# Two joining copies moved behind a weight's casts in ScalarE's queue

## The chip, the core and the metric

The kernel runs on one core of a Trainium2 chip. A core has five engines, each with its own queue of instructions that it takes in order: TensorE (PE; its weight loads are listed apart as PEld), VectorE (DVE), ScalarE (ACT), GpSimd (POOL) and SyncE (SP), which issues the DMA transfers here. Engines wait for one another by semaphores. The metric is the device time of one execution in microseconds (us); lower is better.

## The reference

Two layers of a decoder trunk for 512 tokens of width 1024, in fp32. Each layer has a feed-forward sub-layer, a mixing sub-layer (three kinds of attention, gated and merged) and a second feed-forward sub-layer, all with normalisation before and after:

```
def _swiglu(t, w_gate, w_up, w_down):
    return (jax.nn.silu(t @ w_gate) * (t @ w_up)) @ w_down

for l in range(DEPTH):
    f = _swiglu(_rmsnorm(h, ffn1_pre_g[l]), ffn1_w_gate[l], ffn1_w_up[l], ffn1_w_down[l])
    h = h + 0.5 * _rmsnorm(f, ffn1_post_g[l])
    ...   # mixing
    f = _swiglu(_rmsnorm(h, ffn2_pre_g[l]), ffn2_w_gate[l], ffn2_w_up[l], ffn2_w_down[l])
    h = h + 0.5 * _rmsnorm(f, ffn2_post_g[l])
```

The hidden width of the feed-forward sub-layers is 2816, 22 columns of 128. The change concerns these four feed-forward stages only. In the kernel their names carry `a` (the first of a layer) or `c` (the second).

## The kernel before

**Three matmuls for one.** Every fp32 operand is split into a high part (`wh_...`, `ah...`: rounded to fp32r) and a low part (`wl_...`, `al...`: the rest), and a product is three matmuls: high by high, low by high, high by low (`mm3`, lines 205 to 207). The high part is a cast on ScalarE and the low part a subtraction on VectorE that needs the cast (`split`, lines 182 and 183). The split of a weight tile of 128x1024 is thus a DMA into a raw tile (`raw_...`), a cast and a subtraction. High parts have a ring of four buffers and low parts another ring of four.

**Seven products for eight.** Sixteen of the 22 hidden columns are handled as two blocks (numbers 0 and 1) by a scheme with seven products of half size where eight would be needed. A gate job, an up job and a down job exist for each block and product. A down job (ci, n) is product n of block ci. It has two weight units (`wh_dc_1_1_0` and `wh_dc_1_1_2` are the units of job (1,1) in stage `c`: rows from 0 and from 2), each used by 12 matmuls, so a job is 24 matmuls. The down jobs run in the order

(0,0), (1,0), (0,1), (1,1), (0,2), (1,2), (0,3), (0,4), and so on,

which makes (0,1) the third and (1,1) the fourth. In between stand passes over the six remaining hidden columns, two columns to a weight, one column to a pass of 24 matmuls. Around the change the order on TensorE is: (1,0), gate pass of column 18, (0,1), (1,1), gate pass of column 19, (0,2), up pass of column 18, (1,2). The weights of the two gate passes are the same two units, which hold two of the four buffers until the second pass is over.

**Turning the hidden values.** The up products of a block give a hidden quarter with tokens and features the other way round from what the down jobs need. `turn` (line 796) turns it with the DMA engine, two bytes at a time: two copies on ScalarE part each word into halves (line 807, tiles `th...`), two transposing DMAs turn the halves (line 808, into `tr...`), and two *joining copies* on ScalarE put the words together again in the tile of hidden rows (line 811, into `hr...`). `turn` is called from each later product job. It parts the words in the first job after the quarter is done and joins them two or three jobs later. The last up product of block 1 (product 6) fills the second token half of `hr..._2`. Its joining copies are traced in job (1,1).

**Who needs the joined tile.** The left factor of a down job is a sum of hidden quarters on VectorE, then split (`first_factor`, lines 845 to 851). Line 845 for (1,2), `as..._1_2`, is the first reader of the joined half. The left factor is made one job ahead.

**What sets the order.** The code is traced in the order in which jobs are stepped through, with weights of up to four units loaded ahead of the running job. A scheduler then orders each engine's queue by data dependences and its own estimate of when each instruction is ready. `tc.keep_in_program_order` pins an instruction to the traced order, and `tc.issue_after(ins)` queues what is traced inside it behind `ins` on that engine; it adds an order, not a wait for `ins` to end.

## Time and profile before

| | us |
|---|---|
| median of 3 runs | 2356.36 |
| lowest, highest | 2354.06, 2357.69 |
| the profiled execution, its time | 2354.76 |
| its span on the core | 2353.0 |
| TensorE busy in the span | 2339.6 (99%) |
| VectorE busy | 1798.8 (76%) |
| ScalarE busy | 1505.3 (64%) |

The granted TensorE clock is 0.999 of full speed over the span. A row of a time line has the start in us from the span's start, the duration, the engine, the line, the operation, out<-in by tile names with the buffer numbers left out, the shape, and a count when neighbours of one kind are merged; a bracket gives the idle time of that engine just before, and what ended it. Matmuls overlap, so a duration of 0.39 does not mean that the next one starts 0.39 later: the starts tell the pace.

### The profile page before, as it was taken

How to read it: one execution, taken by the hardware profiler on the slowest of the kernel's cores; microseconds unless marked ns; L12 is line 12 of the kernel's file. 1: busy time of each engine (PE TensorE's matmuls, PEld its weight loads, DVE VectorE, ACT ScalarE, POOL GpSimd, SP SyncE). 2: the span in 40 equal slices, each digit the busy share in tenths (PEclk: the TensorE clock that was granted, in tenths of full speed). 3: DMA queues.
4: the chain of work that ended last, by engine and by line, in shares of the span. 5: the costliest groups of instructions: out<-in, count | busy, mean ns of one | idle time of the engine just before them, and what ended most of it. 6: DMA issues, size and time to landing. Idle time of an engine off the chain costs nothing.

```text
span 2353.0 us, 30931 instructions
## 1 busy us (share of the span) xinstructions
PE 2339.6 (99%) x11623; PEld 1977.7 (84%) x11623; DVE 1798.8 (76%) x2359; ACT 1505.3 (64%) x2302; POOL 75.5 (3%) x134
## 2 busy tenths in 40 slices
PE   9999999999999999999999999999999999999998
PEld 7888888888888888878898888888888888988887
DVE  8877876577777688878798788766677767888785
ACT  6677465576766556774656774655777665667744
POOL 0000000000111000000000000000001100000000
PEclk9999999999999999999999999999999999999999
DMA  6667454223323555674646655532323235566744
GB/s 206 192 178 220 143 197 129 78 83 88 91 72 108 188 188 159 199 188 153 225 145 182 202 176 178 189 108 72 100 72 99 73 124 190 170 189 181 207 145 146
DMA packets 297849, 354.96 MB, mean 151 GB/s; under 512 B 78282, under 2 KB 189154, under 8 KB 297700
## 3 DMA queue, kind: packets, MB, share of 16 engines
q1 hardware_dynamic: 297604, 352.97, 48.8%
q8 instruction: 91, 1.49, 0.3%
q14 instruction: 58, 0.48, 0.1%
q0 software_dynamic: 96, 0.03, 0.0%
HBM read 319.39 MB, written 16.78 MB: 143 GB/s over the span
## 4 chain that ended last, share of the span: by engine, by line
PE 90%; DMA 4%; DVE 2%; ACT 2%; issue 1%; SPq 0%; DVEq 0%; ACTq 0%
PE pg L206 4%; PE pg L205 4%; PE pg L207 4%; PE pda L206 3%; PE pdc L206 3%; PE pda L205 3%; PE pda L207 3%; PE pdc L207 3%; PE pdc L205 3%; PE pb L207 1%; PE pb L206 1%; PE pb L205 1%; PE pq L205 1%; PE pq L206 1%; PE pk L207 1%
## 5 line engine op out<-in xcount | busy, mean ns | idle before, releaser
L205 PE MATMUL pg<-us_a,wh_wg 128*128 128x512 f32 x384 | 151.1, 394 | 0.0
L206 PE MATMUL pg<-us_a,wh_wg 128*128 128x512 f32 x384 | 149.9, 390 | 0.0
L207 PE MATMUL pg<-us_a,wl_wg 128*128 128x512 f32 x384 | 149.9, 390 | 0.0
L183 DVE TENSOR_TENSOR wl_da<-raw_da,wh_da 128x1024 fp32r<-128x1024 f32 x50 | 61.0, 1224 | 46.3 <-ACT wh_da L182 46.1
L183 DVE TENSOR_TENSOR wl_dc<-raw_dc,wh_dc 128x1024 fp32r<-128x1024 f32 x50 | 61.0, 1223 | 44.5 <-ACT wh_dc L182 44.4
L206 PE MATMUL pdc<-wl_dc,ahc 128*128 128x512 f32 x224 | 88.0, 393 | 1.5 <-DVE wl_dc L183 1.5
L206 PE MATMUL pda<-wl_da,aha 128*128 128x512 f32 x224 | 88.0, 393 | 0.3 <-DVE wl_da L183 0.3
L207 PE MATMUL pdc<-wh_dc,alc 128*128 128x512 f32 x224 | 87.3, 390 | 0.0
L207 PE MATMUL pda<-wh_da,ala 128*128 128x512 f32 x224 | 87.3, 390 | 0.0
L205 PE MATMUL pdc<-wh_dc,ahc 128*128 128x512 f32 x224 | 86.7, 390 | 0.4 <-ACT wh_dc L182 0.4
L205 PE MATMUL pda<-wh_da,aha 128*128 128x512 f32 x224 | 86.6, 390 | 0.0
L207 PEld LDWEIGHTS pg<-us_a,wl_wg 128*128 128x128 f32 x384 | 72.1, 188 | 15.1
L205 PEld LDWEIGHTS pg<-us_a,wh_wg 128*128 128x128 f32 x384 | 72.2, 188 | 14.1
L206 PEld LDWEIGHTS pg<-us_a,wh_wg 128*128 128x128 f32 x384 | 72.2, 188 | 14.0
L182 ACT CAST wh_da<-raw_da 128x1024 fp32r<-128x1024 f32 x50 | 52.2, 1049 | 41.5 <-DMA raw_da<-in_ffn_w_down_dram 13.6
L182 ACT CAST wh_dc<-raw_dc 128x1024 fp32r<-128x1024 f32 x50 | 52.1, 1049 | 36.5 <-DMA raw_dc<-in_ffn_w_down_dram 12.2
L186 DVE SCALAR_TENSOR_TENSOR wl_wg<-raw_wg,wh_wg 128x1024 fp32r<-128x1024 f32 x48 | 58.5, 1222 | 21.9 <-ACT wh_wg L185 21.8
L200 DVE SCALAR_TENSOR_TENSOR ga<-pg,bgate,ga 128x512 f32<-128x512 f32 x48 | 35.9, 747 | 50.0 <-ACT ga L199 50.0
L182 ACT CAST wh_uc<-raw_uc 128x1024 fp32r<-128x1024 f32 x44 | 46.3, 1053 | 39.8 <-PE pwc0g L207 9.4
L183 DVE TENSOR_TENSOR wl_uc<-raw_uc,wh_uc 128x1024 fp32r<-128x1024 f32 x44 | 53.7, 1221 | 17.1 <-ACT wh_uc L182 16.9
L185 ACT ACTIVATE wh_wg<-raw_wg 128x1024 fp32r<-128x1024 f32 x48 | 50.5, 1056 | 25.1 <-PE pv L1113 11.7
L182 ACT CAST wh_ua<-raw_ua 128x1024 fp32r<-128x1024 f32 x44 | 46.2, 1052 | 31.1 <-PE pwa0g L207 8.1
(643 smaller groups left out, 8017.3 us busy)
## 6 DMA issues: line engine op xcount, KB each, us to landing
raw_da<-in_ffn_w_down_dram SPq DMA_DIRECT2D x66, 512.0 KB, 4.7
raw_dc<-in_ffn_w_down_dram SPq DMA_DIRECT2D x66, 512.0 KB, 4.3
raw_ga<-in_ffn_w_gate_dram SPq DMA_DIRECT2D x52, 512.0 KB, 4.5
raw_ua<-in_ffn_w_up_dram SPq DMA_DIRECT2D x52, 512.0 KB, 4.7
raw_gc<-in_ffn_w_gate_dram SPq DMA_DIRECT2D x52, 512.0 KB, 4.0
raw_uc<-in_ffn_w_up_dram SPq DMA_DIRECT2D x52, 512.0 KB, 4.0
raw_wg<-in_w_gate_dram SPq DMA_DIRECT2D x48, 512.0 KB, 3.6
raw_wo<-in_w_out_dram SPq DMA_DIRECT2D x24, 512.0 KB, 3.4
```

The source lines that it names most:

```text
L182: both = [nc.scalar.copy(h_ap, src)]
L183: make = lambda: nc.vector.tensor_tensor(l_ap, src, h_ap.bitcast(F32), ALU.subtract)
L185: both = [nc.scalar.activation(h_ap, src, AF.Copy, scale=scale)]
L186: make = lambda: nc.vector.scalar_tensor_tensor(l_ap, src, scale, h_ap.bitcast(F32), ALU.mult, ALU.subtract)
L200: nc.vector.scalar_tensor_tensor(t, z, minus, t, ALU.max, ALU.add)
L205: nc.tensor.matmul(pt, lh, rh, start=start, stop=False, skip_group_check=free)
L206: nc.tensor.matmul(pt, lh, rl, start=False, stop=False, skip_group_check=free)
L207: nc.tensor.matmul(pt, ll, rh, start=False, stop=stop, skip_group_check=free)
```

## The change

The joining copies of the last up product of block 1 (hidden rows 2, second token half) are traced inside `tc.issue_after` of the high part's cast of the last unit of down job (1,1). For this `split` returns its instructions, a unit keeps its cast in `self.cast`, and `products` keeps the last unit of (1,1) in `st["second"]`. All other joining copies stay as they were. Nothing is added to or taken from the program; the order changes in all four feed-forward stages in the same way.

```diff
@@ def split @@
         if Q.pinned:
             for ins in both:
                 tc.keep_in_program_order(ins)
+        return both
@@ class BlockUnit @@
-            self.heir, self.behind = None, False
+            self.heir, self.behind, self.cast = None, False, None
...
-            self.split_from(src)
+            self.cast = self.split_from(src)[0]
             self.loaded()
@@ def turn @@
                 if kk in (0, 1) and age == back:
                     r = hidden_rows(row)[:].bitcast(U16)
-                    nc.scalar.copy(r[:, :, i * S + kk:(i + 1) * S:2].rearrange("p f (e q) -> p e f q", e=2),
-                                   planes[kk].rearrange("p (e f q) -> p e f q", e=2, q=P))
+                    dst_ = r[:, :, i * S + kk:(i + 1) * S:2].rearrange("p f (e q) -> p e f q", e=2)
+                    src_ = planes[kk].rearrange("p (e f q) -> p e f q", e=2, q=P)
+                    last = (row, i) == (2, 1)
+                    with tc.issue_after(st["second"].cast.ins) if last else nullcontext():
+                        nc.scalar.copy(dst_, src_)
@@ def products @@
                 had[ci, n] = uns
+                if (ci, n) == (1, 1):
+                    st["second"] = uns[-1]
                 yield uns, (lambda at=at, uns=uns: product(at, uns))
```

ScalarE's queue in the second feed-forward stage of the first layer, before. `hrc_2` is the joined tile, `trc0u_6_*` the turned halves, `sc_18` the activated gate of column 18, `btc` a kept weight block.

```order
L182 CAST ahc_0_2_9438<-asc_0_2_9440 128x1024
L811 COPY hrc_2_9047<-trc0u_6_0_9316 128x2x4x128
L811 COPY hrc_2_9047<-trc0u_6_1_9317 128x2x4x128
L630 ACTIVATE sc_18_9575<-pgc_18_9350 128x512
L182 CAST wh_dc_1_1_0_9340<-raw_dc_1_1_0_9252 128x1024
L182 CAST wh_dc_1_1_2_9346<-raw_dc_1_1_2_9254 128x1024
L182 CAST wh_dc_0_2_0_9377<-btc_0_0_9286 128x1024
```

And after the change (lines have moved by up to six):

```order
L182 CAST ahc_0_2_9438<-asc_0_2_9440 128x1024
L631 ACTIVATE sc_18_9575<-pgc_18_9350 128x512
L182 CAST wh_dc_1_1_0_9340<-raw_dc_1_1_0_9252 128x1024
L182 CAST wh_dc_1_1_2_9346<-raw_dc_1_1_2_9254 128x1024
L816 COPY hrc_2_9047<-trc0u_6_0_9316 128x2x4x128
L816 COPY hrc_2_9047<-trc0u_6_1_9317 128x2x4x128
L182 CAST wh_dc_0_2_0_9377<-btc_0_0_9286 128x1024
```

The activation and the two casts of (1,1) went ahead of the two copies.

VectorE's queue at the same place, before. `asc_1_2` is the sum that reads the joined tile, `asc_0_2` the running sum of block 0, `alc` a low part of a left factor.

```order
L183 TENSOR_TENSOR wl_dc_1_1_0_9341<-raw_dc_1_1_0_9252,wh_dc_1_1_0_9340 128x1024
L183 TENSOR_TENSOR alc_0_2_9439<-asc_0_2_9440,ahc_0_2_9438 128x1024
L845 TENSOR_TENSOR asc_1_2_9510<-hrc_2_9047,hrc_3_9006 128x1024
L183 TENSOR_TENSOR wl_dc_1_1_2_9347<-raw_dc_1_1_2_9254,wh_dc_1_1_2_9346 128x1024
L327 TENSOR_TENSOR btc_0_0_9286<-btc_0_0_9286,raw_dc_0_2_0_9288 128x1024
L847 TENSOR_TENSOR asc_0_2_9440<-asc_0_2_9440,hrc_0_8445 128x1024
L183 TENSOR_TENSOR wl_dc_0_2_0_9378<-btc_0_0_9286,wh_dc_0_2_0_9377 128x1024
```

And after:

```order
L183 TENSOR_TENSOR wl_dc_1_1_0_9341<-raw_dc_1_1_0_9252,wh_dc_1_1_0_9340 128x1024
L183 TENSOR_TENSOR alc_0_2_9439<-asc_0_2_9440,ahc_0_2_9438 128x1024
L851 TENSOR_TENSOR asc_0_2_9440<-asc_0_2_9440,hrc_0_8445 128x1024
L183 TENSOR_TENSOR wl_dc_1_1_2_9347<-raw_dc_1_1_2_9254,wh_dc_1_1_2_9346 128x1024
L328 TENSOR_TENSOR btc_0_0_9286<-btc_0_0_9286,raw_dc_0_2_0_9288 128x1024
L849 TENSOR_TENSOR asc_1_2_9510<-hrc_2_9047,hrc_3_9006 128x1024
L183 TENSOR_TENSOR wl_dc_0_2_0_9378<-btc_0_0_9286,wh_dc_0_2_0_9377 128x1024
```

The sum that reads the joined tile and the subtraction of block 0's running sum have changed places. On TensorE one matmul of the following gate pass moves ahead of the first low-part matmul of the second unit of (1,1). Further on, ScalarE and VectorE each swap one split of an activation with one of a weight. The queues of SyncE and GpSimd are the same.

More of the change, by code (lines that the diff above doesn't have):

```diff
@@ L1 @@
 import itertools
-from contextlib import ExitStack, contextmanager
+from contextlib import nullcontext, ExitStack, contextmanager
 import concourse.bass as bass
```

## The prediction

> **What bounds the kernel now.** I read the page's busy times first, then TensorE's waits, then time lines of ScalarE, VectorE and TensorE around the joining copies of all four feed-forward stages.

> ```profile
> PE 2339.6 (99%) x11623; PEld 1977.7 (84%) x11623; DVE 1798.8 (76%) x2359; ACT 1505.3 (64%) x2302; POOL 75.5 (3%) x134
> ...
> PE pdc L206 <- DVE wl_dc L183: 1.5, 2, 0.8
> ...
> PE pdc L205 <- ACT wh_dc L182: 0.4, 1, 0.4
> ...
> PE pda L206 <- DVE wl_da L183: 0.3, 1, 0.3
> ```

> The span is 2353.0 us and TensorE is busy for 2339.6 of it, so everything that this change could return lies in 13.4 us of idle time and in matmuls that were stretched. The three waits (in total, times, longest) are of one kind: matmuls of the down jobs wait for the high or low part of a weight. They add to 2.2 us.

> Now the worst place, the second feed-forward stage of the first layer. ScalarE first, then TensorE (start, duration, engine, line, operation; in brackets the idle time and what ended it):

> ```profile
> 1042.05 1.04 ACT L182 CAST ahc<-asc 128x1024 fp32r<-128x1024 f32 x1
> 1042.99 1.35 ACT L811 COPY hrc<-trc0u 128x1024 uint16<-128x1024 uint16 x1
> 1044.69 1.36 ACT L811 COPY hrc<-trc0u 128x1024 uint16<-128x1024 uint16 x1 [0.35 <-DMA trc0u<-thc0u]
> 1045.91 0.59 ACT L630 ACTIVATE sc<-pgc 128x512 f32<-128x512 f32 x1
> 1046.39 1.99 ACT L182 CAST wh_dc<-raw_dc 128x1024 fp32r<-128x1024 f32 x2
> 1053.34 1.05 ACT L182 CAST wh_dc<-btc 128x1024 fp32r<-128x1024 f32 x1 [4.96 <-DVE btc L327]
> ```

> ```profile
> 1041.50 0.39 PE L205 MATMUL pdc<-wh_dc,ahc 128*128 128x512 f32 x1
> ...
> 1044.22 0.39 PE L205 MATMUL pdc<-wh_dc,ahc 128*128 128x512 f32 x1
> ...
> 1047.48 0.50 PE L205 MATMUL pdc<-wh_dc,ahc 128*128 128x512 f32 x1 [0.38 <-ACT wh_dc L182]
> 1048.75 0.50 PE L206 MATMUL pdc<-wl_dc,ahc 128*128 128x512 f32 x1 [0.76 <-DVE wl_dc L183]
> ```

> The two copies at 1042.99 and 1044.69 are the ones the change moves. The two casts at 1046.39 are those of the fourth job, (1,1). TensorE began the third job, (0,1), at 1041.50. It has 24 matmuls, and undisturbed they start 0.2267 us apart: from 1041.50 to 1044.22 there are 12. So (1,1) was due at 1046.94. Its weights were still being cast, and TensorE stood twice. Behind the casts ScalarE is idle for 4.96 us: the copies stand where the weights are urgent, in front of a gap that would hold them.

> **What it costs now.** From the first matmul of (0,1) to the first of the fifth job, (0,2), there are 72 matmuls (24 of each of two jobs, 24 of the gate pass between), 16.32 us at that pace. The rows of both ends, stage by stage (the second stage begins at 1041.50, above):

> ```profile
> 207.86 0.39 PE L205 MATMUL pda<-wh_da,aha 128*128 128x512 f32 x1
> ...
> 224.63 0.39 PE L205 MATMUL pda<-wh_da,aha 128*128 128x512 f32 x1
> ...
> 1059.77 0.39 PE L205 MATMUL pdc<-wh_dc,ahc 128*128 128x512 f32 x1
> ...
> 1375.98 0.39 PE L205 MATMUL pda<-wh_da,aha 128*128 128x512 f32 x1
> ...
> 1393.11 0.39 PE L205 MATMUL pda<-wh_da,aha 128*128 128x512 f32 x1
> ...
> 2208.33 0.39 PE L205 MATMUL pdc<-wh_dc,ahc 128*128 128x512 f32 x1
> ...
> 2225.99 0.39 PE L205 MATMUL pdc<-wh_dc,ahc 128*128 128x512 f32 x1
> ```

> The four differences are 16.77, 18.27, 17.13 and 17.66; less 16.32 each, the losses are 0.45, 1.95, 0.81 and 1.34, together 4.55 us. That is twice the 2.2 us of recorded waits, since a matmul that waited for weights and the one after it also run late. The forecast goes by starts, 4.55; by waits alone the sum would be 2.2. [...]

> **What the change moves, and what then limits the casts.** The first stage, where the copies found their data ready:

> ```profile
> 208.35 2.54 ACT L811 COPY hra<-tra0u 128x1024 uint16<-128x1024 uint16 x2
> 210.75 0.59 ACT L630 ACTIVATE sa<-pga 128x512 f32<-128x512 f32 x1
> 211.23 1.04 ACT L182 CAST wh_da<-raw_da 128x1024 fp32r<-128x1024 f32 x1
> 213.50 1.05 ACT L182 CAST wh_da<-raw_da 128x1024 fp32r<-128x1024 f32 x1 [1.23 <-PE pda L207]
> 218.19 1.05 ACT L182 CAST wh_da<-bta 128x1024 fp32r<-128x1024 f32 x1 [3.63 <-DVE bta L327]
> ...
> 1379.73 1.03 ACT L182 CAST wh_da<-raw_da 128x1024 fp32r<-128x1024 f32 x1
> ...
> 2212.58 1.04 ACT L182 CAST wh_dc<-raw_dc 128x1024 fp32r<-128x1024 f32 x1
> ```

> 1. *The first cast of (1,1)* no longer stands behind 2.54 us of copies. It then waits for its buffer: there are four for high parts, two held by the gate pass, so it takes the one that the first half of (0,1) leaves. What such a release takes is shown by the second cast, at 213.50, while (0,1) ended when (1,1) was due at 207.86 + 24 x 0.2267 = 213.30: 0.20 us later. So the first cast can start at 12 x 0.2267 + 0.20 = 2.92 us after the start of (0,1): 210.78, 1044.42, 1378.90 and 2211.25. It started at 211.23, 1046.39, 1379.73 and 2212.58, that is 0.45, 1.97, 0.83 and 1.33 late: in each stage the loss found above. ScalarE's small activation before it fits (0.59 us, from about 208.35 in the first stage).

> 2. *Is the raw weight there?* It is issued at 203.77 in the first stage and at 1038.41 in the second. The first landed after 4.8 us, at 208.6. For the second the trace gives no landing; the next raw weight there took 6.0.

> ```profile
> 203.77 0.53 SPq L297 DMA_DIRECT2D raw_da<-in_ffn_w_down_dram  x1
> ...
> raw_da<-in_ffn_w_down_dram SPq DMA_DIRECT2D x1, 512.0 KB, 4.8
> ...
> 1038.41 0.53 SPq L297 DMA_DIRECT2D raw_dc<-in_ffn_w_down_dram  x1
> ...
> raw_dc<-in_ffn_w_down_dram SPq DMA_DIRECT2D x1, 512.0 KB, 6.0
> ```

> With 4.8 it is there at 1043.2, with 6.0 at 1044.41, just when the cast can start. No loss is charged. SP's own order is unchanged, and no DMA is added or moved in it.

> 3. *VectorE's low parts.* The first stage's rows:

> ```profile
> 212.31 1.23 DVE L183 TENSOR_TENSOR wl_da<-raw_da,wh_da 128x1024 fp32r<-128x1024 f32 x1 [4.07 <-ACT wh_da L182]
> ...
> 215.72 1.22 DVE L183 TENSOR_TENSOR wl_da<-raw_da,wh_da 128x1024 fp32r<-128x1024 f32 x1
> ...
> 219.27 1.23 DVE L183 TENSOR_TENSOR wl_da<-bta,wh_da 128x1024 fp32r<-128x1024 f32 x1
> ...
> 213.08 0.19 PEld L205 LDWEIGHTS pda<-wh_da,aha 128*128 128x128 f32 x1
> 213.59 0.19 PEld L206 LDWEIGHTS pda<-wl_da,aha 128*128 128x128 f32 x1 [0.32 <-DVE wl_da L183]
> ```

> The first low part runs from 1.08 to 2.31 us after its cast starts, so it ends at 5.23 us after the start of (0,1). TensorE loads it about 0.22 before the matmul that uses it (213.08 for 213.30), at 5.45. Margin: about 0.2 us less a semaphore's 0.05, where before it came 0.32 late. The second low part begins 4.49 after the first cast and ends at 8.63; two operations stand between as before, only another subtraction of the same length in place of the sum that needs the copies. It is wanted after 16 matmuls of (1,1) instead of 15 (the gate matmul moved up), at 5.44 + 3.63 - 0.22 = 8.85. Margin 0.2 again. So both stalls go, by little. If both margins failed by a hair, a stage would keep two restarts of about 0.15 to 0.2 (0.50 against 0.39 in the rows above), 1.4 us over four stages; the gain's lower bound is 4.55 - 1.4 = 3.1, the upper one 4.55.

> 4. *The copies themselves.* They start when the second cast ends, at 5.44 + 0.20 + 0.95 = 6.6 us after the start of (0,1), and end at 9.2: in the first stage at 217.0, inside the idle 3.63 us before 218.19. The cast behind them waits for VectorE's subtraction anyway, which now ends at 9.8 (the cast began at 218.19, 10.3). VectorE's operations follow 1.14 apart (212.31 to 215.72 is three of them), so after the second low part, begun at 7.4, the subtraction begins at 8.55 and the sum that needs the copies at 9.7: margin 0.5. Behind it the low part for (0,2) ends by 12.2, and (0,2) starts at 16.3: margin 4. So 4 x 2.54 us of copies cost nothing here. If this cover went (the second cast held 5 us longer), TensorE would wait at (0,2).

> 5. *The swap of one activation's cast with a weight cast further on* and the gate matmul that changed places with a down matmul leave counts and lengths the same: nothing.

> **Sum.** 4 stages: -(0.45 + 1.95 + 0.81 + 1.34) = -4.55 us. The profiled execution took 2354.76 (span 2353.0 and 1.76 around it), so it would take 2350.2. The median of the three runs is 2356.36, 1.6 longer. Against it, 2351.8 follows if those 1.6 us lie elsewhere, and 2350.2 if they are larger stalls here. The second stage's stall hangs on a transfer that ScalarE waits for (0.35 in its row), and such a landing differs from run to run, so some of it is likely: I take 0.4 and forecast 2351.4, 0.21% below the median.

> **Rivals.**
> - *Only part returns.* The two margins of 0.2 us fail and short stalls stay: gain 3.1, 2353.3. For it: the margins are thin. Against it: the steps behind them are equally long in all four stages.
> - *Nothing returns.* The raw weight of (1,1), not the buffer, is late, as the copies' own data was in the second stage; or a later wait takes the time back: about 2356. Against it: the landing of 4.8, and no wait recorded on TensorE between (0,2) and the stage's end.
> - *Slower.* The copies now stand behind a cast that waits for TensorE, and everything behind them on ScalarE waits too; VectorE, in order, stands at the sum that needs them. It decides once the copies end later than 9.7 + 4 = 13.7 us after the start of (0,1), 4.5 later than worked out; at 7 us later, four stages would lose 4 x 2.5 = 10 and gain 4.55: 2361.8. The row for it is the second cast's wait for TensorE (1.23). Against it: that wait ended 0.20 us after (0,1), and nothing shows it longer. [...]

> **How the numbers follow.** Forecast 0.70, partly 0.16, nothing 0.06, slower 0.08. Measured medians of this kernel lie within 2354.06 to 2357.69, so about 0.2%, 4.7 us, is what a measurement tells from no change, and the forecast, -5.0, lies right at it. Of the forecast's 0.70 I put 0.47 beyond 0.2% and 0.23 within, of the partial case 0.03 and 0.13; nothing is within. That gives 0.50 faster, 0.42 same, 0.08 slower. The range reaches from 2349.5 (2350.2 and some scatter) to 2355.0 (the partial case and as much).

> **What would show it.** Right: the first cast of (1,1) starts 2.9 us after (0,1) in all stages; the 72 matmuls take 16.3 to 16.5; TensorE's waits for low parts of down weights are gone from the list; the copies start at about 6.6 and the waits of the cast after them shrink from 3.6 to 5.0 us to about 0.5. Wrong: the first cast waits for a DMA; TensorE waits at (0,2) or for the second low part; or the first cast already waited for its buffer before, so that it starts no earlier.

## The result and the profile after

The changed kernel takes 2350.83 us (median of 10 runs, 2348.70 to 2352.04); the kernel before, 2356.48 beside it (10 runs, 2354.06 to 2359.56). The ratio is 0.9976, with a 95% interval of 0.9966 to 0.9986: faster by 3.3 to 8.0 us. The forecast was 2351.4. The profiled execution took 2351.63 (span 2349.9), against 2354.76 (2353.0) before.

The profile page's busy times of the changed kernel, and its list of TensorE's waits, down to the shortest that it names (in total, times, longest):

```profile
PE 2337.9 (99%) x11623; PEld 1977.6 (84%) x11623; DVE 1799.9 (77%) x2359; ACT 1506.5 (64%) x2302; POOL 75.5 (3%) x134
...
PE pwo L207 <- DVE wl_wo L183: 1.3, 2, 1.0
PE warm L1588 <- DVE warm L1682: 1.3, 1, 1.3
PE gqx L529 <- DMA grow<-in_ffn_pre_g_dram: 0.8, 1, 0.8
PE pga L662 <- ACT w_ga L182: 0.5, 1, 0.5
PE mt L1064 <- DVE mraw L1057: 0.5, 1, 0.5
PE pwa0g L206 <- ACT pwa0g L755: 0.4, 1, 0.4
```

The three waits of down jobs (`pdc`, `pda`) that led the list before are gone. The work itself has not changed: the same counts, and busy times within 2 us. ScalarE's time line of the changed kernel in the second feed-forward stage, where the worst place was:

```profile
1042.95 1.05 ACT L182 CAST ahc<-asc 128x1024 fp32r<-128x1024 f32 x1
1043.90 0.59 ACT L631 ACTIVATE sc<-pgc 128x512 f32<-128x512 f32 x1
1044.99 1.05 ACT L182 CAST wh_dc<-raw_dc 128x1024 fp32r<-128x1024 f32 x1 [0.51 <-PE pdc L208]
1047.67 1.06 ACT L182 CAST wh_dc<-raw_dc 128x1024 fp32r<-128x1024 f32 x1 [1.62 <-PE pdc L208]
1048.63 2.57 ACT L816 COPY hrc<-trc0u 128x1024 uint16<-128x1024 uint16 x2
1052.31 1.05 ACT L182 CAST wh_dc<-btc 128x1024 fp32r<-128x1024 f32 x1 [1.11 <-DVE btc L328]
```

Both casts of (1,1) now wait for TensorE to free a buffer, and the copies run between the second cast and the next one, which waits 1.11 us for VectorE where it had waited 4.96.

The loss is the time from the first matmul of (0,1) to the first of (0,2), less the 16.32 us that 72 matmuls take undisturbed. The changed kernel's rows at both ends, in the four stages:

```profile
208.59 0.39 PE L206 MATMUL pda<-wh_da,aha 128*128 128x512 f32 x1
...
225.06 0.39 PE L206 MATMUL pda<-wh_da,aha 128*128 128x512 f32 x1
...
1042.03 0.39 PE L206 MATMUL pdc<-wh_dc,ahc 128*128 128x512 f32 x1
...
1058.51 0.39 PE L206 MATMUL pdc<-wh_dc,ahc 128*128 128x512 f32 x1
...
1374.04 0.39 PE L206 MATMUL pda<-wh_da,aha 128*128 128x512 f32 x1
...
1390.51 0.39 PE L206 MATMUL pda<-wh_da,aha 128*128 128x512 f32 x1
...
2206.47 0.39 PE L206 MATMUL pdc<-wh_dc,ahc 128*128 128x512 f32 x1
...
2222.94 0.39 PE L206 MATMUL pdc<-wh_dc,ahc 128*128 128x512 f32 x1
```

Each stage takes 16.47 us (16.48 in the second, by rounding), so 0.15 is lost in each, 0.60 in all, where the kernel before lost 4.55 in its profiled execution. That is 3.95 us returned at the four places. The two profiled executions differ by only 3.13. Most of the missing 0.82 was there before the first place: (0,1) of the first stage begins at 208.59 here and 0.73 earlier, at 207.86, before, and up to that point the two programs do the same work. In the runs below that start lies anywhere from 207.03 to 209.02, so this is scatter.

### The profile page after: what moved, and what is told of

It reads as the page before. It is cut to its first block, busy times and chain, and to the rows that moved or that the text cites. A ratio compares the mean times of both kernels' runs of the same rounds, so it can differ in the third digit from the quotient of the medians.

```text
span 2349.9 us, 30935 instructions
## 1 busy us (share of the span) xinstructions
PE 2337.9 (99%) x11623; PEld 1977.6 (84%) x11623; DVE 1799.9 (77%) x2359; ACT 1506.5 (64%) x2302; POOL 75.5 (3%) x134
## 4 chain that ended last, share of the span: by engine, by line
PE 89%; DVE 3%; DMA 3%; ACT 3%; issue 2%; SPq 0%; DVEq 0%; ACTq 0%
PE pg L207 3%; PE pg L206 3%; PE pg L208 3%; PE pda L207 3%; PE pdc L207 3%; PE pda L206 3%; PE pda L208 3%; PE pdc L208 3%; PE pdc L206 3%; PE pq L207 1%; PE pq L206 1%; PE pk L207 1%; PE pb L208 1%; PE pk L208 1%; PE pq L208 1%
## 5 line engine op out<-in xcount | busy, mean ns | idle before, releaser
L206 PE MATMUL pg<-us_a,wh_wg 128*128 128x512 f32 x384 | 150.9, 393 | 0.0
L207 PE MATMUL pg<-us_a,wh_wg 128*128 128x512 f32 x384 | 149.7, 390 | 0.0
L183 DVE TENSOR_TENSOR wl_da<-raw_da,wh_da 128x1024 fp32r<-128x1024 f32 x50 | 61.0, 1224 | 44.3 <-ACT wh_da L182 44.2
L183 DVE TENSOR_TENSOR wl_dc<-raw_dc,wh_dc 128x1024 fp32r<-128x1024 f32 x50 | 61.0, 1224 | 42.3 <-ACT wh_dc L182 42.3
L207 PE MATMUL pdc<-wl_dc,ahc 128*128 128x512 f32 x224 | 87.7, 391 | 0.0
L207 PE MATMUL pda<-wl_da,aha 128*128 128x512 f32 x224 | 87.6, 391 | 0.0
L206 PE MATMUL pdc<-wh_dc,ahc 128*128 128x512 f32 x224 | 86.5, 389 | 0.0
L206 PE MATMUL pda<-wh_da,aha 128*128 128x512 f32 x224 | 86.5, 389 | 0.0
L207 PEld LDWEIGHTS pg<-us_a,wh_wg 128*128 128x128 f32 x384 | 72.2, 188 | 14.1
L206 PEld LDWEIGHTS pg<-us_a,wh_wg 128*128 128x128 f32 x384 | 72.1, 188 | 14.1
L182 ACT CAST wh_da<-raw_da 128x1024 fp32r<-128x1024 f32 x50 | 52.3, 1051 | 45.6 <-PE pda L208 14.3
L182 ACT CAST wh_dc<-raw_dc 128x1024 fp32r<-128x1024 f32 x50 | 52.3, 1049 | 43.0 <-PE pdc L208 14.1
L182 ACT CAST wh_uc<-raw_uc 128x1024 fp32r<-128x1024 f32 x44 | 46.3, 1053 | 38.4 <-PE pwc0g L208 9.1
L182 ACT CAST wh_ua<-raw_ua 128x1024 fp32r<-128x1024 f32 x44 | 46.2, 1053 | 31.7 <-PE pwa1g L208 8.6
L183 DVE TENSOR_TENSOR wl_uc<-raw_uc,wh_uc 128x1024 fp32r<-128x1024 f32 x44 | 53.8, 1222 | 16.2 <-ACT wh_uc L182 16.0
## 6 DMA issues: line engine op xcount, KB each, us to landing
raw_da<-in_ffn_w_down_dram SPq DMA_DIRECT2D x66, 512.0 KB, 4.8
raw_dc<-in_ffn_w_down_dram SPq DMA_DIRECT2D x66, 512.0 KB, 4.3
raw_ga<-in_ffn_w_gate_dram SPq DMA_DIRECT2D x52, 512.0 KB, 4.5
raw_ua<-in_ffn_w_up_dram SPq DMA_DIRECT2D x52, 512.0 KB, 4.5
raw_gc<-in_ffn_w_gate_dram SPq DMA_DIRECT2D x52, 512.0 KB, 4.2
raw_uc<-in_ffn_w_up_dram SPq DMA_DIRECT2D x52, 512.0 KB, 4.0
raw_wg<-in_w_gate_dram SPq DMA_DIRECT2D x48, 512.0 KB, 3.6
raw_wo<-in_w_out_dram SPq DMA_DIRECT2D x24, 512.0 KB, 3.4
```

The source lines that it names most:

```text
L182: both = [nc.scalar.copy(h_ap, src)]
L183: make = lambda: nc.vector.tensor_tensor(l_ap, src, h_ap.bitcast(F32), ALU.subtract)
L206: nc.tensor.matmul(pt, lh, rh, start=start, stop=False, skip_group_check=free)
L207: nc.tensor.matmul(pt, lh, rl, start=False, stop=False, skip_group_check=free)
```

## The experiments

The prediction's account is that the copies stood in front of the casts of (1,1), that the ring of four buffers is the next limit, and that the copies cost nothing in ScalarE's gap. The other accounts to be told from it are that part of the difference is scatter, that the thin margins on VectorE fail, and that the place of the copies behind the second cast matters in itself. The losses of all profiled executions, worked out as above, with the start of the first cast of (1,1) after that of (0,1):

| kernel | loss, stages 1 to 4 | sum | first cast |
|---|---|---|---|
| before | 0.45, 1.95, 0.81, 1.34 | 4.55 | 3.37, 4.89, 3.75, 4.25 |
| before again | 1.95, 2.27, 1.22, 1.27 | 6.71 | 4.88, 5.22, 4.16, 4.16 |
| before, third | 0.79, 2.31, 0.75, 1.56 | 5.41 | 3.74, 5.22, 3.69, 4.50 |
| changed | 0.15, 0.15, 0.15, 0.15 | 0.60 | 2.96 in all |
| changed again | 0.71, 0.16, 0.15, 0.16 | 1.18 | 3.52, then 2.96 |
| low part first | 0.00 in all | 0.00 | 2.96 in all |
| copies between the casts | 0.55, 0.25, 0.25, 0.25 | 1.30 | 3.26, then 2.96 |
| copies far behind | 0.18, 0.16, 0.15, 0.17 | 0.66 | 2.99, then 2.96 |
| copies twice, old place | 6.69, 6.71, 4.77, 5.39 | 23.56 | 7.29, 7.56, 6.31, 6.96 |
| copies twice, new place | 0.15, 0.16, 0.16, 0.15 | 0.62 | 2.96 in all |

**The kernel before, two more times** (no edit).

> The kernel before, unchanged, profiled once more. Theory V (the four stalls differ from run to run, since the copies in front of the casts wait for transposing transfers): the 72 matmuls from the start of (0,1) to the start of (0,2) take other times than 16.77, 18.27, 17.13 and 17.66 us, and their summed loss over 16.32 each differs from 4.55 by over 0.5 us. Rival F (the stalls are fixed, and the median's larger gain is scatter from elsewhere): the sum is 4.55 within 0.3 us. The time ratio to before is 1.000 within 0.001 by both.

> The kernel before, profiled a third time, for how far the stalls scatter. Theory V: the sum of the four losses lies between 4 and 8 us and differs from 4.55 and 6.71; where the first cast starts late, the copies in front of it start late too, and the latest of them waits for a transposing transfer. Rival F: one of the two profiles so far was an exception, and this one repeats the other within 0.3.

Measured: 2355.73 in five rounds (ratio 1.0002, 0.9993 to 1.001), and one execution of 2354.07. Their losses were 6.71 and 5.41, so three executions of one program lost 4.55 to 6.71, by whatever ScalarE met ahead of the copies. The second stage lost most in all three (1.95, 2.27 and 2.31), and there the second moved copy waited 0.35, 0.28 and 0.30 us for its transposing DMA. In the first stage of "before again", an earlier joining copy (product 5's) waited for its transposing DMA. ScalarE's time line there:

```profile
206.21 1.35 ACT L811 COPY hra<-tra0u 128x1024 uint16<-128x1024 uint16 x1 [1.59 <-DMA tra0u<-tha0u]
207.44 1.04 ACT L182 CAST wh_da<-raw_da 128x1024 fp32r<-128x1024 f32 x1
208.38 0.58 ACT L885 COPY pda<-pda 128x512 f32<-128x512 f32 x1
208.90 1.04 ACT L182 CAST aha<-asa 128x1024 fp32r<-128x1024 f32 x1
209.84 2.56 ACT L811 COPY hra<-tra0u 128x1024 uint16<-128x1024 uint16 x2
212.25 0.59 ACT L630 ACTIVATE sa<-pga 128x512 f32<-128x512 f32 x1
212.74 2.00 ACT L182 CAST wh_da<-raw_da 128x1024 fp32r<-128x1024 f32 x2
```

From 206.21 to 214.7 ScalarE has no gap, so the 1.59 us reached the casts almost whole: the first began 4.88 us after (0,1) instead of 3.37. The stall is made of everything in that queue, the two moved copies (2.54) being the part that need not stand there.

**The changed kernel again** (no edit).

> The changed kernel, profiled once more. Theory V: the casts of (1,1) now hang on TensorE's buffer alone, so the 72 matmuls take 16.47 us in all four stages, within 0.05, as in its first profile. Rival F expects the same here. Time: 4.0 to 5.6 us below before, ratio 0.9976 to 0.9983.

Measured: 2350.43 beside 2355.24, ratio 0.9976 (0.9966 to 0.9985). Three stages lost 0.15 to 0.16, as expected. The first lost 0.71, which was not expected. ScalarE's time line there:

```profile
207.01 1.35 ACT L816 COPY hra<-tra0u 128x1024 uint16<-128x1024 uint16 x1 [1.75 <-DMA tra0u<-tha0u]
...
209.18 0.58 ACT L889 COPY pda<-pda 128x512 f32<-128x512 f32 x1
...
211.55 1.05 ACT L182 CAST wh_da<-raw_da 128x1024 fp32r<-128x1024 f32 x1 [0.33 <-ACT sa L631]
```

The same earlier joining copy waited 1.75 us for its DMA. The copy of `pda` behind it came late for TensorE, which went 0.65 us from one matmul to the next within (0,1) (its list of waits has 0.3 us of that). The end of (0,1)'s first half moved with it, and so did the cast that needs its buffer: it began at 3.52. So TensorE lost this time to the copy of `pda`, not to a late cast of (1,1). The delay cost 0.56 us more than in a quiet stage, where in "before again", with the two copies behind it, it took the stage from 0.45 to 1.95.

**The second low part ahead of block 0's subtraction.**

```diff
@@ class BlockUnit @@
-            self.cast = self.split_from(src)[0]
+            self.cast, self.low = self.split_from(src)
@@ def first_factor @@
             elif n == 3:
-                nc.vector.tensor_tensor(s, s, a(0, 0), ALU.subtract)
+                with tc.issue_after(st["second"].low.ins) if ci == 0 else nullcontext():
+                    nc.vector.tensor_tensor(s, s, a(0, 0), ALU.subtract)
```

> The changed kernel with the subtraction of block 0's running sum queued on VectorE behind the low part of the second unit of (1,1). Theory (the 0.15 us left in each stage are TensorE's wait for that low part, made late by two dependent subtractions in front of it): the low part starts about 0.6 to 1.0 us earlier against the start of (0,1), TensorE's weight load waits for it no more, and the 72 matmuls take 16.32 us; 0.6 us less over four stages, which a timing can't tell. Rival (the 0.15 us are the price of the gate matmuls that stand among the down matmuls): still 16.47.

Measured: 2350.49, ratio 0.9979 (0.997 to 0.9988). The second low part begins 6.73 us after (0,1), 1.09 earlier than in the changed kernel, and the loss is 0.00 in all four stages, so the 0.15 that the change leaves is VectorE's second low part. How it came late, by the changed kernel's VectorE and its weight loads (the second stage; (0,1) began at 1042.03):

```profile
1046.08 1.23 DVE L183 TENSOR_TENSOR wl_dc<-raw_dc,wh_dc 128x1024 fp32r<-128x1024 f32 x1 [2.30 <-ACT wh_dc L182]
1047.44 1.23 DVE L183 TENSOR_TENSOR alc<-asc,ahc 128x1024 fp32r<-128x1024 f32 x1
1048.70 1.23 DVE L851 TENSOR_TENSOR asc<-asc,hrc 128x1024 f32<-128x1024 f32 x1
1049.85 1.22 DVE L183 TENSOR_TENSOR wl_dc<-raw_dc,wh_dc 128x1024 fp32r<-128x1024 f32 x1
```

```profile
1051.12 0.19 PEld L207 LDWEIGHTS pdc<-wl_dc,ahc 128*128 128x128 f32 x1 [0.28 <-DVE wl_dc L183]
```

The starts are 1.36, 1.26 and 1.15 apart, not 1.14 each. In the kernel before the second of these operations followed the first at once:

```profile
213.45 1.22 DVE L183 TENSOR_TENSOR ala<-asa,aha 128x1024 fp32r<-128x1024 f32 x1
214.59 1.22 DVE L845 TENSOR_TENSOR asa<-hra,hra 128x1024 f32<-128x1024 f32 x1
```

There the first low part was at 212.31, 1.14 ahead. The subtraction overwrites the tile that `alc` has just read, and starts 1.26 after it in all four stages; where an independent sum follows `al...`, as in the rows just shown, it is 1.14. For the 1.36 the program has a wait on TensorE in front of `alc`. The starts fit it: `alc` begins 5.41 us after (0,1) in every undisturbed stage, 0.42 after the last matmul but one of (0,1) starts (22 x 0.2267 = 4.99). That one is the last to read the high part of (0,1)'s left factor, and 0.43 is also what lies between the start of (0,1)'s last matmul (5.21) and the cast that takes over its weight's buffer (5.64). Where (0,1) itself was held up by 0.3 or 0.56 `alc` began 0.30 or 0.56 later. In the kernel before, `al...` came at 5.59 or later and had nothing to wait for. That the buffer is what it waits for is argued from these starts; no run gave it another buffer.

The time is not to be told from the changed kernel's: 0.6 us is less than the intervals.

**The copies between the two casts.**

```diff
                 if (ci, n) == (1, 1):
-                    st["second"] = uns[-1]
+                    st["second"] = uns[0]
```

> The changed kernel with the copies queued behind the first unit's cast of (1,1) in place of the second's: they stand between the two casts, and VectorE's order is that of before. Theory (the first cast alone, which stood behind the copies, made the stall): the first cast starts 2.96 us after (0,1) in all stages, the copies fill the time in which the second cast waits for its buffer, the second cast starts about 0.8 us later than in the changed kernel, and of the 4.55 us lost before at most 1.2 stay: 72 matmuls in 16.4 to 16.6 us. Rival (both casts, or VectorE's new order, are needed): the stalls come back in part, 16.7 us or more.

Measured: 2351.66, ratio 0.9983 (0.9974 to 0.9991). Most of the gain needs only the first cast ahead of the copies. ScalarE in the second stage, where (0,1) began at 1041.82:

```profile
1044.78 1.05 ACT L182 CAST wh_dc<-raw_dc 128x1024 fp32r<-128x1024 f32 x1 [0.72 <-ACT sc L631]
1045.74 2.58 ACT L816 COPY hrc<-trc0u 128x1024 uint16<-128x1024 uint16 x2
1048.17 1.06 ACT L182 CAST wh_dc<-raw_dc 128x1024 fp32r<-128x1024 f32 x1
```

The copies fill the time in which the second cast waits anyway, and hold it up by 0.71 (6.35 for 5.64). That by itself costs nothing, since VectorE would not have come to the second low part sooner. The loss is 0.25 a stage, 0.10 over the change. Its low part begins 7.69 us after (0,1), 0.13 earlier than in the changed kernel, but TensorE's order has one gate matmul less ahead of it and wants it 0.23 earlier: 0.10 worse. In the first stage an earlier joining copy waited 1.47 for its DMA, and 0.55 was lost.

**The moved copies done twice, at the old place.**

```diff
-                    nc.scalar.copy(r[...], planes[kk]...)
+                    for _ in range(2 if (row, i) == (2, 1) else 1):
+                        nc.scalar.copy(r[...], planes[kk]...)
```

> The kernel before with each of the two joining copies done twice, at their old place (extra work; the values stay the same). ScalarE gets 4 x 2.44 = 9.8 us more in both this run and the next. Theory (what counts is how late the first cast of (1,1) starts; each us beyond the slack of 0.4 is a us on TensorE): the first cast starts 2.44 later in each stage, at 6 to 7.5 us after (0,1), and the time rises by 4 x 2.44 = 9.8 us, by 9 to 10.5. Rival (ScalarE is 64% busy and absorbs it): within 2 us of before.

Measured: 2371.63 against 2356.04, 15.6 us longer (ratio 1.0067, 1.0052 to 1.0082), and a loss of 23.56. The direction is as expected, the size is not. (The profiled execution, 2375.18, was the longest of the four of this kernel, so its 23.56 is more than the medians' difference and the 5.56 of before make up.) ScalarE, then TensorE, in the first stage, where (0,1) began at 209.02:

```profile
211.03 4.93 ACT L812 COPY hra<-tra0u 128x1024 uint16<-128x1024 uint16 x4
215.83 0.58 ACT L630 ACTIVATE sa<-pga 128x512 f32<-128x512 f32 x1
216.31 1.98 ACT L182 CAST wh_da<-raw_da 128x1024 fp32r<-128x1024 f32 x2
```

```profile
217.40 0.79 PE L205 MATMUL pda<-wh_da,aha 128*128 128x512 f32 x1 [2.71 <-ACT wh_da L182]
218.66 0.80 PE L206 MATMUL pda<-wl_da,aha 128*128 128x512 f32 x1 [0.47 <-DVE wl_da L183]
219.25 0.63 PE L207 MATMUL pda<-wh_da,ala 128*128 128x512 f32 x1
219.68 0.63 PE L205 MATMUL pda<-wh_da,aha 128*128 128x512 f32 x1
...
223.09 0.63 PE L207 MATMUL pda<-wh_da,ala 128*128 128x512 f32 x1
```

The last matmul of (0,1) starts at 214.30, so the first gap is 3.10 for 0.23, and the second 1.26 for 0.23: 2.87 and 1.03 lost. Over the four stages these two terms are 2.87, 3.21, 1.96 and 2.62, and four times 1.03: 14.8 us, 9.2 more than the mean loss of the three executions of the kernel before (5.56). That is the term which the doubled copies were to add. The other 8.8 us come after the second matmul, nearly all with 0.43 from one matmul to the next where 0.23 is usual. The view by windows has the granted clock for it (a row: the window and its length, busy time and count of PE, PEld, DVE, ACT and POOL, then the granted clock, the DMA share and GB/s):

```profile
209.00:217.40 8.40, 5.69 (x26) 4.32 (x24) 1.25 (x2) 8.40 (x10) 3.10 (x5) 1.00 0.65 218
217.40:223.90 6.50, 6.04 (x13) 4.42 (x14) 6.50 (x6) 0.99 (x2) 0.00 (x0) 0.50 0.30 85
224.30:230.00 5.70, 5.70 (x27) 4.70 (x26) 3.78 (x4) 4.12 (x6) 0.00 (x0) 1.00 0.56 182
```

After the pause TensorE ran at half clock for at least these 6.5 us. The kernel before comes near it without reaching it: its longest pause at the four places, in the second stage of "before again" (and in that of the third execution), is 1.10 and then 1.26 from matmul to matmul, and the clock there stays full:

```profile
1048.00:1052.00 4.00, 2.52 (x10) 1.59 (x9) 2.95 (x3) 1.97 (x3) 0.00 (x0) 1.00 0.54 168
```

**The moved copies done twice, at the new place.**

```diff
                     with tc.issue_after(st["second"].cast.ins) if last else nullcontext():
-                        nc.scalar.copy(dst_, src_)
+                        for _ in range(2 if last else 1):
+                            nc.scalar.copy(dst_, src_)
```

> The changed kernel with each of the two moved copies done twice, at their new place (extra work; the values stay the same). Theory (there they lie in ScalarE's wait for VectorE and under 4 us of slack): the copies end at about 11.6 us after (0,1), the sum that needs them starts there instead of at 10.1, the low part for (0,2) still comes over 2 us early, the 72 matmuls take 16.47 as with single copies, and the time is that of the changed kernel within 1 us. Rival of the slower case (copies behind a waiting cast soon hold up the fifth job): up to 9.8 us more.

Measured: 2353.93, ratio 0.9991 (0.9982 to 1.0001), some 3.1 us over the changed kernel. At the four places the loss is 0.62, as expected, but the time is not within 1 us of the changed kernel's: the cost appears later. The VectorE sum that reads the joined tile, and a matmul of the second unit of (1,2), in the second stage:

```profile
1053.19 1.23 DVE L850 TENSOR_TENSOR asc<-hrc,hrc 128x1024 f32<-128x1024 f32 x1 [1.46 <-ACT hrc L817]
```

```profile
1072.71 0.50 PE L207 MATMUL pdc<-wl_dc,ahc 128*128 128x512 f32 x1 [0.68 <-DVE wl_dc L183]
```

The copies end 11.6 us after (0,1), and the sum, in VectorE's queue ahead of the later weight subtractions, waits 1.46 for them. These subtractions then free their raw buffers later. SyncE's issues of the next four raw weights (durations in ns, first and last start), in this kernel and in the changed one:

```profile
L298 SPq DMA_DIRECT2D raw_dc<-in_ffn_w_down_dram x4: 368/415/468, 1060.2 to 1062.9; - x4
```

```profile
L298 SPq DMA_DIRECT2D raw_dc<-in_ffn_w_down_dram x4: 367/416/469, 1059.3 to 1062.0; - x4
```

They start 18.6 us after (0,1) (at 1041.56) for 17.3 (at 1042.03). TensorE waits for a low part at (1,2). At that matmul and the few behind it the starts, compared one by one, slip against the changed kernel's by 0.47, 0.87, 0.37 and 1.25 in the four stages, 2.96 together, about the 3.1 of the medians. The waiting sum is not the only way there. On ScalarE the cast of (0,2)'s first weight stands behind the doubled copies and began 11.46 us after (0,1), where in the changed kernel it began at 10.28; without the sum, this alone would have held up its low part almost as much. Further on, ScalarE's order also differs in this kernel (the cast of the next left factor ahead of a weight's), so the share of each was not measured.

**The copies behind the second cast of (0,2).**

```diff
-                if (ci, n) == (1, 1):
+                if (ci, n) == (0, 2):
                     st["second"] = uns[-1]
```

> The changed kernel with the copies queued behind the second unit's cast of the fifth job, (0,2), instead of (1,1): some 8 us further back, and VectorE's order then has the low parts of (0,2) ahead of the sum that needs the copies. Theory (only the place ahead of the casts of (1,1) cost time; the first job that needs the joined tile is (1,2), 27 us after (0,1)): 72 matmuls in 16.3 to 16.5 us, no new wait up to (1,2), the changed kernel's time within 1 us. Rival (the place found is a narrow one): stalls at (0,2) or (1,2), 2 us or more each stage.

Measured: 2352.07, ratio 0.9985 (0.9976 to 0.9995), which overlaps the changed kernel's interval. Its median is 1.2 us over the changed kernel's, a little outside the 1 us expected; the profiled execution, 2350.30, is one of the two shortest of ten and lost 0.66 at the four places, with no new wait up to (1,2), so whether this place costs something stays open. The copies now run at 1055.89 and 1058.06, 15.7 and 17.9 us after (0,1), far behind the end at 11.6 that cost 3 us in the run above. Here VectorE's order has changed with them:

```profile
1055.07 1.23 DVE L183 TENSOR_TENSOR wl_dc<-btc,wh_dc 128x1024 fp32r<-128x1024 f32 x1 [1.17 <-ACT wh_dc L182]
...
1059.45 1.23 DVE L849 TENSOR_TENSOR asc<-hrc,hrc 128x1024 f32<-128x1024 f32 x1
```

The scheduler set the sum behind both low parts of (0,2) (the second is the upper row), and on ScalarE the copies stand behind both casts of (0,2): the first began at 10.28, as in the changed kernel. So nothing that (0,2) needs stood behind the copies or behind the sum that waits for them. The two runs together say that copies as late as this need not cost 3 us, and that what is queued behind them decides; which of the two queues did it in the run above, they don't separate.

## Why the prediction was right

**The sum.** The forecast of 2351.4 is 0.6 over the median. It rested on a loss of 4.55, found from the starts of matmuls and not from TensorE's 2.2 us of recorded waits, and on 0.4 us for stalls that are larger in other executions. The losses before were 4.55, 6.71 and 5.41, mean 5.56; after, 0.60 and 1.18, mean 0.89. The difference is 4.7 us, against 4.8 (2355.24 to 2350.43) and 5.65 (2356.48 to 2350.83) by the medians. Up to 1 us of the second is left to scatter; the runs don't say more. Going by starts was right, and the allowance for variation was too small by about 0.6 (5.56 less 4.55 is 1.0, not 0.4). By luck this offsets the 0.60 that the low parts kept back (step 3), so the forecast's nearness to the median is better than its working.

**Step 1, the first cast.** Right: forecast at 2.92 us after (0,1), measured 2.96 in all four stages. Its row names TensorE as what ended the wait in the first two; in the other two it names nothing, and the same start to 0.01 us speaks for the same cause. What it left out is that (0,1) itself can be held up on its way: in one of the two executions of the changed kernel an earlier joining copy's DMA made the copy of `pda` late, and with (0,1) the cast of the first stage moved to 3.52.

**Step 2, the raw weight.** Right: the cast that needs it starts at 2.96 in every quiet stage, and no row of it names a DMA.

**Step 3, the low parts.** Right on the first, wrong on the second. Forecast to begin 7.4 us after (0,1), end at 8.63 and be in time by 0.2, it began at 7.82, ended at 9.04 and was late. The failed term is VectorE's pace of 1.14 carried over from the rows before: there the left factor's low part never had to wait for TensorE, and the operation behind it was another one. With the first low part moved ahead, that wait came to light (0.22 us), and the subtraction put in place of the sum, which overwrites what the low part reads, costs 0.12 (1.26 for 1.14). The price, 0.15 a stage, is the lower end of the 0.15 to 0.2 that the prediction gave for one restart. So the rival in which part returns was right on one of its two margins; it kept 0.60 us back, where it was priced at 1.4 for both.

**Step 4, the copies.** Right that they cost nothing: they start at 6.6 and the low part of (0,2) is in time. The sum begins at 10.09 (forecast 9.7), behind copies that end at 9.17; the cast behind them waits 1.11, not 0.5, since VectorE came later. Wrong in the margin: the prediction put the point where the copies begin to cost at 4 us beyond the sum, at (0,2). Copies that ended 2.4 us later than in the changed kernel already cost 3 us, and did so at (1,2), where the raw weights had been asked for 1.3 us later.

**Step 5, the swaps.** Nothing was seen of them in the changed kernel's own trace: TensorE has no wait for them in its list. The gate matmul that moved ahead did count, in the prediction's favour: it gave the second low part 0.23 us, as the run with the copies between the casts shows.

**The rivals.** "Nothing" fell with the first cast's start, 2.96 for 3.37 to 5.22. "Slower" fell with the new wait of the second cast (1.62), which ended at 5.64 in every quiet stage.

## What to carry to other kernels

Where an engine that takes its queue in order stands idle behind urgent work (here ScalarE, 4.96 us behind the casts of (1,1)), look at what stands in front of that work: a copy whose result is wanted later, ahead of a cast that is wanted now, costs the critical engine whatever part of its length goes beyond the cast's own slack (here about half of the copies' 10.2 us). Measure the stall by the starts of the matmuls against their undisturbed pace, in more than one execution, since the same queue lost 4.55 to 6.71 us. Before carrying an engine's pace into a new order, ask of each operation which wait it had already outlasted in the old one, and follow a delay past the first consumer to the buffers that it frees.

## What was not expected of the hardware

**The landing of a transposing DMA moves a stage's loss.** The same joining copy found its data ready in five of the ten profiled executions and waited 1.47 to 1.75 us for it in the other five. In the first stage of the kernels with the copies moved, such a wait cost 0.03, 0.30 and 0.56 us; with the copies still behind it, in "before again", 1.5.
